# The low part of k as a tile per head with doubled rows, in a two-block transformer of split float32 products

## The chip, the core and the metric

One NeuronCore of one Trainium2 chip runs the whole program in one launch. The metric is device time in microseconds (us), the median of several executions; the kernel before takes 2513.65 us (median of 3, 2512.61 to 2514.68). All inputs and outputs are float32.

## What is computed

512 tokens of 1024 features pass through two blocks. The first has three branches: a forgetting attention of 12 heads of 64 (causal, with a decay taken from gates), a complex diagonal state space model, and attention over 256 memory tokens. The second block is two layers, each with a full attention (8 query heads, 2 key heads of 64), a dilated attention and an MLP of 4096. The change touches the logits of the forgetting and of the dilated attention. Cut to that:

```python
# forgetting attention, per head (12 heads of 64)
s = q @ k.T / 8 + F[:, None] - F[None, :]
s = where(key <= query, s, -1e30)
y = softmax(s) @ v
# dilated attention, per layer: 4 heads of 64 and three groups of (window, dilation)
for (w, d) in ((128, 1), (512, 4), (2048, 16)):
    s = q_g @ k_g.T / 8            # keys at multiples of d within w / 2 of the query
    ...
# the three groups' softmaxes are merged by their log-sum-exp
```

## The kernel before

Every operand of a large product is split into two parts in a rounded float32 format: hi, the rounded value, and lo, the rest. A weight product is three products into one accumulator: hi hi, hi lo, lo hi (`mm3`, L106 to L110; L124 to L126 with tokens as rows). Weights come in pieces of 512 KB: loaded by SP's queue (`fetch`), hi cast by ACT (L88), lo subtracted by DVE or POOL in turn (L90).

A head's logits come twice. The query-major part (`s_item`) makes the row maximum and takes the first product of the pair alone; the key-major part (`t_item`, L365) makes the weights: logits into PSUM (`region_mm`, products at L311), exponential (L379) and cast (L381) on ACT, the low part on DVE (L383), then three products with the values (L400 to L402). In it a head's logits are two products, given by `pairs`:

```python
(qx, own), (kh, kl) = q, k
return [(qx, kh), (qx[own], kl[own])]
```

qx holds hi of q in the head's own 64 rows and lo in the other 64, and kh holds hi of k in both halves, so the first product, with 128 rows, is (q hi + q lo) times k hi. The second is q hi times k lo: 64 rows, 0 to 63 for the first head of a pair and 64 to 127 for the second. `put` (L639) makes these tiles from a finished block of two heads: ACT casts hi (L650), POOL copies it into the other half (L672), DVE subtracts lo (L656). One tile kl serves both heads of a pair, each head in its own rows.

Full attention (`both`) has its own tiles: its second product takes a tile k2, with 128 rows, and is named q,k in the profile. A forgetting unit is two heads with four key blocks each, so 8 products on kl, six units in all. A dilated unit is two heads, each with two tiles of four regions of 128 columns and four tiles of 192 or 256 columns: 24 products on kl; there are two units in each of the two layers. A region in these stretches is the pair, then a bf16 product for the mask (and for the decay, names FM, FF, fk); a key-major tile of the dilated attention begins with a bf16 product for the maximum (L375).

What sets the order: lists of items that `merge` and `mix` deal out among the projections (`layer`: the first dilated unit's key-major items among the branch product `ba`, the second's among the first five gate blocks `gb`), work in the background by `tick`, and behind this a scheduler that reorders the instructions of every engine. Activations live in one ring of 73 tiles of 128x512 (`u`).

Of the kernel before, what the change touches and what calls it, by code (L numbers as in the profile page):

```python
# [10 lines left out]
F32R = mybir.dt.float32r  # L11
# [12 lines left out]
def f32(t):  # L24
    return t.bitcast(F32)


class Core:
# [17 lines left out]
    def u(self, dt=F32, name="u"):  # L46
        """a [128, 512] tile of four-byte words from the common ring."""
        self.n += 1
        return self.ring.tile([128, T], dt, tag="u", name=f"{name}_{self.n}", bufs=self.NU)
# [5 lines left out]
    def psum(self, cfg):  # L55
        """(re)divide the eight PSUM banks"""
        self.psx.close()
        self.PSB = cfg
        self.psx = ExitStack()
        self.n += 1  # L60
        self.ps = self.psx.enter_context(self.tc.tile_pool(name=f"ps{self.n}", bufs=1, space=PSUM))
        self.ctx.push(self.psx)
# [30 lines left out]
    def get(self, name, kb):  # L93
        """the next piece: hi and lo as [128, kb, columns]."""
        i = self.iw
        assert self.strips[i][0] == name, (self.strips[i][0], name)
        for j in range(i, i + self.NW[1]):
            self.split(j)
        for j in range(i + self.NW[1], i + self.NW[1] + self.NW[0]):
            self.fetch(j)  # L100
        self.iw += 1
        n = self.strips[i][1].shape[-1]
        return tuple(t[:, 0:n].rearrange("p (k c) -> p k c", k=kb) for t in self.hl.pop(i))

# [7 lines left out]
    def fm(self, out, w, c0, act, kb):  # L112
        """feature-major block: out[128 features, tokens] from strip columns c0..c0+128."""
# [4 lines left out]
    def tm(self, out, ws, act, tok, cols=slice(0, 256)):  # L118
        """token-major block: out[128 tokens, cols]; ws: pieces that follow one another along k."""
# [34 lines left out]
    @staticmethod  # L154
    def half(t, hf):
        """half of the tokens: of four blocks of 128 in order, two."""
# [3 lines left out]
    def halfp(t, hf):  # L160
        """the first or second half of the tokens, in the order (t mod 4, t div 4)."""
        return t.rearrange("p (r i) -> p r i", r=4)[:, :, 64 * hf:64 * hf + 64]

    def sq_acc(self, xj, j, c=slice(0, T), name="sacc", scale=1.0):
        """sum of squares of the feature blocks, by columns."""
# [11 lines left out]
    def sumcols(self, pq, sacc, cols):  # L177
        """pq[:, i]: sums over features of the tokens of 128-blocks; cols: lists of first columns that add up."""
# [4 lines left out]
    def bcast(self, r):  # L183
        """columns r [128, n] -> [128, n * 128] in PSUM, the same in every row."""
# [7 lines left out]
    def rstd(self, sacc, cols):  # L192
        """broadcast of 1/sqrt(mean + eps), in PSUM."""
# [10 lines left out]
    def hsplit(self, src, bias=None, out=None):  # L204
        """hi, lo of src (+ bias)."""
# [20 lines left out]
class Att(Core):  # L226
    """Softmax attention on split operands. A head's logits come twice: query-major for the row
    maximum, key-major for the weights that multiply V and a block of ones, which sums them."""

    @staticmethod  # L230
    def cut(t, c):
        """columns c of t: a slice, or (i0, i1) for those of the tokens 4 i + r in the order (r, i)."""
# [5 lines left out]
    def byblock(t):  # L238
        """t, tokens 4 i + r in blocks of 128 and within these in the order (r, i), as [p, r, block, i]."""
# [3 lines left out]
    def like(t, c):  # L243
        """t in the shape of the columns c."""
        return t if isinstance(c, slice) else t.rearrange("p (r i) -> p r i", r=4)

    def split3(self, dst, src, nsh):
        """dst[..., i] (bf16, i = 0..2) add up to src (float32)."""
# [15 lines left out]
    def turn(self, mc, psum_tag):  # L264
        """columns [128 tokens, 4, 128] -> rows [128, 512] in PSUM (exact)."""
# [5 lines left out]
    def rows(self, mc, tag, psum_tag, out=None):  # L271
        """the same as bf16 in SBUF; of these the last 32 if out is given."""
# [9 lines left out]
    def unit(self, nh, sregs, tregs, qk, vsl, dst, extra=None, nq=4, hd=64, orow=None, fold=None):  # L282
        """Items of a unit of nh heads (pairs of heads share 128 rows of output).
        sregs(qb): tiles of regions (c0, n, piece, q slice, k slice, mask)
        tregs(): tiles of (regions, [(v piece, kb, columns)])
        fold(j): the tile whose other half takes the rows of -max (else these come by a product of their own)
        qk(j, piece) -> pairs (q, k); vsl(j, piece, kb) -> (hi, lo); dst(j) -> (tile AP rows, row0)"""
# [118 lines left out]
        def vrow(j):  # L406
            """rows of a head's values in its sum; the other half holds the sum of the weights."""
# [41 lines left out]
    def mix(a, b, z=1.0):  # L449
        """a and b as one list, spread evenly, b over the first part z."""  # L450
# [3 lines left out]
    def merge(self, a, b):  # L454
        """run items of a with those of b spread evenly among them."""
# [13 lines left out]
class Blk2(Att):  # L469
    def ada_gen(self, l):  # L470
        """columns [128, 48] of silu(c) @ w_ada[l] + b_ada[l]."""
# [6 lines left out]
        def fin(acc, c):  # L478
            """acc: rows of two parts, c and c + 1"""
# [36 lines left out]
    def load2(self):  # L516
        """constants of the second block"""
# [21 lines left out]
    def norm(self, x, gcols, shcols, h):  # L539
        """by half of the tokens: hi and lo of rms(x) * g + shift. Returns the stages stat, hi, lo."""  # L540
# [24 lines left out]
    def head(self, names, h, posts, norm, view, byw=False):  # L565
        """the first blocks behind a norm, a half of the tokens at a time."""
# [26 lines left out]
    def tail(self, name, act, posts):  # L593
        """the last two blocks before a norm, a half of the tokens at a time."""
# [44 lines left out]
    def put(self, o, isq, dst, scale=None, both=False, byblock=False):  # L639
        """stacks of two heads: q -> [hi;lo]; k -> [hi;hi] and lo in the rows of the head. both: q -> [hi;lo] and hi with  # L640
        the other half left to -max; k -> [hi;hi] and lo with ones for it, for heads of either half."""
# [17 lines left out]
        kl = None  # L659
        for h, (own, oth) in enumerate(((A, B), (B, A))):  # L660
# [23 lines left out]
            if kl is None:  # L684
                kl = self.u(F32R, "kl")
            low(v(kl[own]), o[own], v(f32(hi)[own]))
            dst(h, (hi, kl))
# [7 lines left out]
    def pairs(q, k):  # L695
        """operand pairs whose products make up a head's logits"""
        (qx, own), (kh, kl) = q, k
        return [(qx, kh), (qx[own], kl[own])]
# [12 lines left out]
    def block(self, w, c0, act, kb, post):  # L711
        """one feature-major block; post(psum) may return a generator of later stages."""
# [12 lines left out]
    def strip(self, name, act, kb, posts):  # L725
        """items of feature-major blocks."""
# [12 lines left out]
    def v3(self, nb=4):  # L739
        """hi/lo token-major value tiles [128 keys, nb blocks, 128]."""  # L740
        return tuple(self.u(F32R, "v").rearrange("p (b d) -> p b d", b=nb) for _ in range(2))

    def v_new(self):
        """token-major values of two heads, in two tiles of two key blocks: hi as [v0, 1, 1, v1], lo as [v0, 0, 0, v1]."""
# [8 lines left out]
    def v_put(self, V, src, b0, nb):  # L753
        """src: [128, nb, 128], key blocks from b0."""
# [10 lines left out]
    def tm_items(self, name, act, ncol, evac):  # L765
        """token-major strip: 4 token blocks."""
# [15 lines left out]
    def layer(self, l, norm, view, x, out=None):  # L782
        """norm(h, mod, ada): the stages that fill h; x: the residual tiles (filled by then).
        Returns the new tiles, their squares accumulated, or writes out."""
# [28 lines left out]
        def vpost(key, byblock=False):  # L813
            """values of a feature-major block, transposed"""
# [191 lines left out]
def plan1(out, g, W):  # L1006
    """strips of the first block after u"""
# [45 lines left out]
class Blk1(Blk2):  # L1053
# [21 lines left out]
    def exact_exp(self, out, x):  # L1075
        """exp to float32's accuracy: 2^k * p(x - k ln 2)."""
# [31 lines left out]
    def s5_setup(self):  # L1108
# [21 lines left out]
        # turns, in two parts: uh * t is exact for t < 512  # L1130
# [37 lines left out]
        # powers of a: [., re/im, k, 24]; of its conjugate (k = 0..3) and, for the inputs, k = 4..1  # L1168
# [17 lines left out]
        # four steps at once: phase 4 * (uh + ul), magnitude mag^4  # L1186
# [8 lines left out]
    def s5_mul(self, dst, x, pw, j):  # L1195
        """x * a^k of four pairs, block diagonal: dst[., (pair, k, group, 16)]; rows of a group only in its columns."""
# [15 lines left out]
    def s5_batch(self, j, U, y):  # L1212
        """four pairs of groups, four steps at a time. The state that enters a step is scanned in a frame that
        turns with it; inputs of the same four steps act through a triangular block matrix."""
# [5 lines left out]
        # phases  # L1220
# [13 lines left out]
        # input matrices  # L1234
# [48 lines left out]
        # output matrices  # L1283
# [59 lines left out]
    def forget(self, h, W, bf):  # L1343
# [15 lines left out]
        # ln((1 + a) / 2) = 2 atanh((a - 1) / (a + 3))  # L1359
# [47 lines left out]
    def gate_items(self, name, n, h, G):  # L1407
        """G[j] = z (1 + tanh(z / 2)), twice the gate."""
# [19 lines left out]
    def branch_items(self, br, name, kb, h, y, merged):  # L1428
        """gates run a strip ahead of the projections"""
# [140 lines left out]
    def mem_load(self):  # L1570
        """mem in four tiles of two feature blocks; sums of squares of the even and of the odd blocks."""
# [6 lines left out]
    def mem_prep(self, xm, sacc):  # L1578
        """hi, lo of the normed memory, and the items that fill them."""
# [92 lines left out]
    def s5_out(self, h, ge, ges, merged):  # L1672
# [55 lines left out]
        def norm(h, mod, ada):  # L1728
            """the final norm, and behind it the first one of the next block:
            rms(y) of y = x g r is r sqrt(mean((x g)^2))."""  # L1730
# [45 lines left out]
def cols_of(v):  # L1776
    """[n*128] -> [128, n]"""
# [3 lines left out]
def strips_of(w, kb):  # L1781
    """[kb*128, n*256] -> [n, 128, kb, 256]"""
# [66 lines left out]
def strip_plan(A):  # L1849
    """(name, array, kb) of every weight strip in the order of use; A: the inputs by name, or None for names only."""  # L1850
# [42 lines left out]
def pieces(A):  # L1893
    """(name, array [128, kb * columns] or None, kb, kb * columns) of every piece, in the order of use."""
# [137 lines left out]
```

## Time and profile before

| | |
|---|---|
| median of 3 runs | 2513.65 us (2512.61 to 2514.68) |
| the profiled execution: span, first to last instruction | 2516.8 us (the page gives no other time for it) |
| TensorE products busy | 2388.2 us, 95% of the span, 12162 products |
| TensorE weight loads | 1978.9 us, 79% |
| DVE / ACT / POOL | 61% / 41% / 32% |
| DMA | 265 MB, mean 105 GB/s |
| granted TensorE clock, mean | 0.969 |

How to read it: a product's busy span runs from its start to its modelled end, and the spans of neighbours overlap, so a busy TensorE is not one at its peak; the distance between the starts of products that follow each other tells what one costs. The granted clock is 1.00 at 2.4 GHz and 0.50 at 1.2 GHz. PE is TensorE's products, PEld its weight loads, DVE VectorE, ACT ScalarE, POOL GpSimd, SP the engine that issues the loads.

### The profile page before, as it was taken

How to read it: one execution, taken by the hardware profiler on the slowest of the kernel's cores; microseconds unless marked ns; L12 is line 12 of the kernel's file. 1: busy time of each engine (PE TensorE's matmuls, PEld its weight loads, DVE VectorE, ACT ScalarE, POOL GpSimd, SP SyncE). 2: the span in 40 equal slices, each digit the busy share in tenths (PEclk: the TensorE clock that was granted, in tenths of full speed). 3: DMA queues.
4: the chain of work that ended last, by engine and by line, in shares of the span. 5: the costliest groups of instructions: out<-in, count | busy, mean ns of one | idle time of the engine just before them, and what ended most of it. 6: DMA issues, size and time to landing. Idle time of an engine off the chain costs nothing. (4 is left out here: it accounts for less than half of the span.)

```text
span 2516.8 us, 32068 instructions
## 1 busy us (share of the span) xinstructions
PE 2388.2 (95%) x12162; PEld 1978.9 (79%) x12162; DVE 1533.0 (61%) x2394; ACT 1038.1 (41%) x1639; POOL 812.3 (32%) x601
## 2 busy tenths in 40 slices
PE   7999989989998889999999999998999999999999
PEld 6876778767888777787787888886777777888888
DVE  7667766666998887555459663258864726522222
ACT  4445543452333447533333423433663423423432
POOL 2445354634221552142122121227311612222121
PEclk9999999999998999998899999999999979999999
DMA  5311113213674321121138553233111313222232
GB/s 183 98 47 55 57 61 108 94 59 135 237 264 172 113 76 51 51 85 66 50 102 301 176 209 101 93 114 99 59 51 50 93 34 117 84 94 99 93 101 84
DMA packets 105610, 265.28 MB, mean 105 GB/s; under 512 B 13664, under 2 KB 23408, under 8 KB 105456
## 3 DMA queue, kind: packets, MB, share of 16 engines
q1 hardware_dynamic: 104304, 261.47, 31.2%
q8 instruction: 96, 1.57, 0.3%
q10 hardware_dynamic: 1152, 1.77, 0.2%
q14 instruction: 58, 0.48, 0.1%
HBM read 244.69 MB, written 9.44 MB: 101 GB/s over the span
## 5 line engine op out<-in xcount | busy, mean ns | idle before, releaser
L108 PE MATMUL pmm<-h,wh 128*128 128x512 f32 (+1 forms) x2232 | 855.7, 385 | 14.7 <-ACT h L213 3.9
L110 PE MATMUL pmm<-h,wl 128*128 128x512 f32 (+1 forms) x2232 | 852.9, 382 | 3.7 <-POOL wl L90 2.8
L109 PE MATMUL pmm<-l,wh 128*128 128x512 f32 (+1 forms) x2232 | 853.4, 383 | 0.0
L90 POOL TENSOR_TENSOR wl<-wr,wh 128x1024 fp32r<-128x1024 f32 (+1 forms) x173 | 422.5, 2442 | 1315.4 <-ACT wh L88 1094.4
L88 ACT CAST wh<-wr 128x1024 fp32r<-128x1024 f32 (+1 forms) x346 | 358.2, 1036 | 928.5 <-PE pmm L109 726.4
L108 PEld LDWEIGHTS pmm<-h,wh 128*128 128x128 f32 x2232 | 424.5, 190 | 96.7 <-ACT h L213 4.8
L110 PEld LDWEIGHTS pmm<-h,wl 128*128 128x128 f32 x2232 | 424.5, 190 | 82.5 <-POOL wl L90 3.8
L109 PEld LDWEIGHTS pmm<-l,wh 128*128 128x128 f32 x2232 | 425.2, 191 | 76.5 <-DVE l L221 0.7
L90 DVE TENSOR_TENSOR wl<-wr,wh 128x1024 fp32r<-128x1024 f32 (+1 forms) x173 | 225.1, 1301 | 168.9 <-ACT wh L88 166.5
L383 DVE TENSOR_TENSOR pl<-pe,ph 128x512 fp32r<-128x512 f32 (+4 forms) x168 | 121.7, 733 | 139.7 <-ACT ph L381 138.9
L961 DVE SCALAR_TENSOR_TENSOR x<-pmm,ada,x 128x512 f32<-128x512 f32 (+1 forms) x100 | 64.2, 643 | 213.9 <-PE pmm L110 213.7
L311 PE MATMUL ps<-qk,qk 128*128 128x512 f32 (+4 forms) x416 | 147.9, 386 | 16.1 <-POOL qk L672 9.6
L505 DVE SCALAR_TENSOR_TENSOR adacc<-adw,cact,adacc 128x512 f32<-128x512 f32 x168 | 154.3, 928 | 3.2 <-DMA adw<-in_wada 0.3
L221 DVE TENSOR_TENSOR l<-r,h 128x512 fp32r<-128x512 f32 x64 | 59.3, 928 | 121.6 <-ACT h L213 121.3
L379 ACT ACTIVATE pe<-ps 128x512 f32<-128x512 f32 (+4 forms) x168 | 84.5, 503 | 80.8 <-PE ps L311 72.7
L311 PEld LDWEIGHTS ps<-qk,qk 128*128 128x128 f32 x416 | 83.1, 204 | 37.7 <-POOL qk L672 11.5
L108 PE MATMUL pmm<-yh,wh 128*128 128x512 f32 (+1 forms) x244 | 94.1, 389 | 3.9 <-ACT yh L1403 2.4
L110 PE MATMUL pmm<-yh,wl 128*128 128x512 f32 (+1 forms) x244 | 93.7, 386 | 0.0
L109 PE MATMUL pmm<-yl,wh 128*128 128x512 f32 (+1 forms) x244 | 93.0, 382 | 0.0
L381 ACT CAST ph<-pe 128x512 fp32r<-128x512 f32 (+4 forms) x168 | 88.8, 528 | 9.4 <-DVE pl L383 3.5
L402 PE MATMUL ppv<-pl,v 128*128 128x512 f32 (+2 forms) x216 | 79.0, 366 | 4.1 <-DVE pl L383 4.0
L400 PE MATMUL ppv<-ph,v 128*128 128x512 f32 (+2 forms) x216 | 79.0, 366 | 2.7 <-ACT ph L381 1.6
(365 smaller groups left out, 3863.2 us busy)
## 6 DMA issues: line engine op xcount, KB each, us to landing
wr<-in_w SPq DMA_DIRECT2D x324, 512.0 KB
adw<-in_wada SPq DMA_DIRECT2D x192, 256.0 KB
xs<-xg SPq DMA_DIRECT2D x136, 64.0 KB
wr<-in_w SPq DMA_DIRECT2D x22, 384.0 KB
xd<-x SPq DMA_DIRECT2D x16, 256.0 KB
x<-xd SPq DMA_DIRECT2D x16, 256.0 KB
x<-in_x SPq DMA_DIRECT2D x16, 128.0 KB
x<-in_x SPq DMA_DIRECT2D x8, 256.0 KB
```

Source lines behind the costliest of these rows:

```text
L88: self.nc.scalar.copy(h[:, 0:n], r[:, 0:n])
L90: eng.tensor_tensor(out=l[:, 0:n], in0=r[:, 0:n], in1=f32(h)[:, 0:n], op=ALU.subtract)
L108: mm(out, wh, ah, start=start, stop=False)
L109: mm(out, wh, al, start=False, stop=False)
L110: mm(out, wl, ah, start=False, stop=stop)
L311: mm(outs[i] if len(r.shape) == 2 else outs[i].rearrange("p (r i) -> p r i", r=r.shape[1]), w, r, start=first and i == 0, stop=last and i ...
L379: nc.scalar.activation(out=e[:, w], in_=pt[:, w], func=AF.Exp)
L381: nc.scalar.copy(ph[:, w], e[:, w])
L383: nc.vector.tensor_tensor(out=pl[:, w], in0=e[:, w], in1=f32(ph)[:, w], op=ALU.subtract)
L400: mm(self.cut(pv, c), vh, h, start=f, stop=False)
L402: mm(self.cut(pv, c), vh, lo, start=False, stop=z)
L505: nc.vector.scalar_tensor_tensor(out=acc, in0=w, scalar=cc, in1=acc, op0=ALU.mult, op1=ALU.add)
```

## The change

Every head gets a kl tile of its own. DVE writes its low part into the head's own 64 rows as before, and POOL copies these into the other 64 rows. `pairs` then gives the whole tiles, so the second product has 128 rows: (q hi + q lo) times k lo, which takes in the product of the two low parts as well. Comments and texts that go from the source shift the line numbers behind them by one.

```diff
-        kl = None
         for h, (own, oth) in enumerate(((A, B), (B, A))):
...
-            if kl is None:
-                kl = self.u(F32R, "kl")
+            kl = self.u(F32R, "kl")
             low(v(kl[own]), o[own], v(f32(hi)[own]))
+            nc.gpsimd.tensor_scalar(out=kl[oth], in0=f32(kl)[own], scalar1=1.0, scalar2=0.0, op0=ALU.mult, op1=ALU.add)
             dst(h, (hi, kl))
...
         (qx, own), (kh, kl) = q, k
-        return [(qx, kh), (qx[own], kl[own])]
+        return [(qx, kh), (qx, kl)]
```

TensorE, DVE, ACT and SP have as many instructions as before; POOL has 642 rows in its order instead of 606. The scheduler moves instructions on every engine but SP.

POOL, the first pair of heads of the forgetting attention (qk is the tile of hi, wl the low part of a weight piece, FF and v are filled with constants). Before:

```order
L1383 MEMSET FF 128x1024
L90 TENSOR_TENSOR wl_896<-wr_664,wh_895 128x1024
L672 TENSOR_SCALAR qk_926<-qk_926 64x512
L672 TENSOR_SCALAR qk_931<-qk_931 64x512
L90 TENSOR_TENSOR wl_1164<-wr_833,wh_1163 128x1024
```

With the change:

```order
L1382 MEMSET FF 128x1024
L90 TENSOR_TENSOR wl_896<-wr_664,wh_895 128x1024
L671 TENSOR_SCALAR qk_926<-qk_926 64x512
L685 TENSOR_SCALAR kl_929<-kl_929 64x512
L671 TENSOR_SCALAR qk_932<-qk_932 64x512
L685 TENSOR_SCALAR kl_935<-kl_935 64x512
L90 TENSOR_TENSOR wl_1167<-wr_833,wh_1166 128x1024
```

The copy of the first head's kl stands ahead of the second head's copy of hi, and both copies of kl ahead of the next weight piece.

POOL, the last projections ahead of the second dilated unit of layer 0. Before:

```order
L672 TENSOR_SCALAR qk_10429<-qk_10429 64x512
L672 TENSOR_SCALAR qk_10434<-qk_10434 64x512
L90 TENSOR_TENSOR wl_10588<-wr_10320,wh_10587 128x1024
L672 TENSOR_SCALAR qk_10471<-qk_10471 64x512
L749 MEMSET v_10647 128x2x128
```

With the change:

```order
L671 TENSOR_SCALAR qk_10459<-qk_10459 64x512
L671 TENSOR_SCALAR qk_10465<-qk_10465 64x512
L685 TENSOR_SCALAR kl_10462<-kl_10462 64x512
L685 TENSOR_SCALAR kl_10468<-kl_10468 64x512
L90 TENSOR_TENSOR wl_10624<-wr_10347,wh_10623 128x1024
L671 TENSOR_SCALAR qk_10504<-qk_10504 64x512
L671 TENSOR_SCALAR qk_10510<-qk_10510 64x512
```

Two copies of kl stand ahead of the weight piece and of the last two copies of hi; the last two copies of kl come after the fills that follow.

TensorE, the first key-major tile of the first dilated unit of layer 0 (ppv: products with the values of the full attention; c the constants of the mask). Before:

```order
L311 MATMUL ps_9677<-qk_8636,kl_8783 128x128
L311 MATMUL ps_9677<-qk_8636,qk_8780 128x128
L400 MATMUL ppv_9501<-ph_9536,v_8028 128x512
L401 MATMUL ppv_9501<-ph_9536,v_8032 128x512
L311 MATMUL ps_9677<-qk_8636,kl_8783 128x128
L311 MATMUL ps_9677<-qk_8636,qk_8780 128x128
L402 MATMUL ppv_9501<-pl_9538,v_8028 128x512
L311 MATMUL ps_9677<-qk_8636,kl_8783 128x128
L311 LDWEIGHTS c_3_68
```

With the change:

```order
L311 MATMUL ps_9704<-qk_8657,qk_8801 128x128
L311 MATMUL ps_9704<-qk_8657,kl_8804 128x128
L311 LDWEIGHTS c_3_68
L311 MATMUL ps_9704<-c_3_68 128x512
L400 MATMUL ppv_9528<-ph_9534,v_8046 128x512
L401 MATMUL ppv_9528<-ph_9534,v_8050 128x512
```

The four pairs of the tile now follow one another, and the products with the values come behind the mask. In the second dilated unit of each layer TensorE's order of key-major tiles and products with the values is the same, row for row.

## Rows read from the trace of the kernel before

**Rows 1.** The page, busy time, share of the span and instructions.

```profile
PE 2388.2 (95%) x12162; PEld 1978.9 (79%) x12162; DVE 1533.0 (61%) x2394; ACT 1038.1 (41%) x1639; POOL 812.3 (32%) x601
```

**Rows 2.** Windows: us, busy time per engine, granted clock, DMA share, GB/s.

```profile
116.00:330.00 214.00, 202.77 (x1094) 155.70 (x1094) 159.58 (x251) 110.42 (x200) 99.65 (x103) 0.98 0.17 56
1035.00:1080.00 45.00, 45.00 (x235) 34.57 (x235) 20.37 (x27) 19.33 (x38) 6.03 (x3) 1.00 0.15 48
1180.40:1186.20 5.80, 5.80 (x28) 3.91 (x27) 1.92 (x2) 3.08 (x5) 0.00 (x0) 1.00 0.36 126
1186.20:1210.10 23.90, 23.90 (x83) 18.52 (x83) 4.35 (x9) 9.78 (x24) 0.00 (x0) 0.50 0.00 1
1885.00:1935.00 50.00, 50.00 (x244) 38.22 (x243) 19.59 (x27) 19.87 (x38) 6.27 (x3) 0.93 0.14 48
...
2036.10:2066.80 30.70, 30.70 (x101) 23.27 (x102) 5.47 (x11) 11.46 (x26) 0.00 (x0) 0.50 0.05 16
```

**Rows 3.** Windows of the products on kl alone: busy time, count, granted clock.

```profile
1186.20:1210.10 23.90, 7.04 (x14) 0.50 0.00 1
...
2036.10:2066.80 30.70, 8.92 (x18) 0.50 0.05 16
```

**Rows 4.** Line L311: count, shortest, median and longest ns, first and last start.

```profile
L311 PE MATMUL ps<-qk,kl x144: 322/380/687, 116.1 to 2073.6; 64*128 64x128 f32 x76, 64*128 64x256 f32 x28, 64*128 64x192 f32 x16, 64*128 64x512 f32 x12
```

**Rows 5.** Timeline of TensorE, second dilated unit of layer 0: start, us, form.

```profile
1180.76 0.32 PE L311 MATMUL ps<-qk,kl 64*128 64x128 f32 x1
1181.01 0.33 PE L311 MATMUL ps<-qk,qk 128*128 128x128 f32 x1
1181.27 0.32 PE L311 MATMUL ps<-qk,kl 64*128 64x128 f32 x1
```

**Rows 6.** Timeline of TensorE's weight loads, full attention and second dilated unit.

```profile
946.37 0.19 PEld L311 LDWEIGHTS ps<-q,k 128*128 128x128 f32 x1
...
1181.27 0.18 PEld L311 LDWEIGHTS ps<-qk,kl 64*128 64x128 f32 x1
```

**Rows 7.** Timeline of TensorE, products that all have 128 rows.

```profile
946.36 0.40 PE L311 MATMUL ps<-qk,qk 128*128 128x512 f32 x1
946.60 0.40 PE L311 MATMUL ps<-q,k 128*128 128x512 f32 x1
...
1213.83 0.28 PE L401 MATMUL ppv<-ph,v 128*128 128x128 f32 x1
...
1214.06 0.27 PE L400 MATMUL ppv<-ph,v 128*128 128x128 f32 x1
```

**Rows 8.** Timeline of TensorE in the forgetting attention.

```profile
115.78 0.39 PE L311 MATMUL ps<-qk,qk 128*128 128x512 f32 x1
...
116.53 0.39 PE L311 MATMUL ps<-FM,fk 128*128 128x512 bf16 x1
...
203.50 0.36 PE L311 MATMUL ps<-qk,qk 128*128 128x256 f32 x1
204.10 0.28 PE L311 MATMUL ps<-FM,fk 128*128 128x256 bf16 x1
```

**Rows 9.** Timeline of TensorE at the lower clock, second dilated unit.

```profile
1190.32 0.41 PE L400 MATMUL ppv<-ph,v 128*128 128x128 f32 x1
1190.53 0.41 PE L401 MATMUL ppv<-ph,v 128*128 128x128 f32 x1
...
1192.71 0.47 PE L311 MATMUL ps<-qk,kl 64*128 64x128 f32 x1
...
1193.52 0.47 PE L311 MATMUL ps<-qk,kl 64*128 64x128 f32 x1
```

**Rows 10.** Copies of hi, subtraction of kl (page's groups and line), waits of TensorE.

```profile
L672 POOL TENSOR_SCALAR qk<-qk 64x512 fp32r<-64x512 f32 x40 | 34.9, 873 | 52.1 <-ACT qk L650 35.3 <-PE ps L311 13.3 <-PE pmm L109 0.9
...
L656 DVE TENSOR_TENSOR kl<-xg,qk x24: 672/690/1019, 933.6 to 2003.5; 64x512 fp32r<-64x512 f32 x24
...
PE ps L311 <- POOL qk L672: 9.6, 5, 2.2
```

## The prediction

> **What bounds the kernel now.** I read the page first: TensorE is busy 95% of a span of 2516.8 us [rows 1], so a term counts if it is TensorE's own time, or a wait that TensorE must sit through. Then the busy times by stage, over the five stretches in which the product that is changed occurs [rows 2]. The reader is to see that TensorE is busy for the whole of the stretches of dilated attention (45.00 of 45.00 us, 23.90 of 23.90, 50.00 of 50.00, 30.70 of 30.70), while no engine behind TensorE is busy there for more than 54% of a stretch (ACT, 3.08 of 5.80), and that two of them ran with the granted clock at 0.50, the lower level of 1.2 GHz, although TensorE had been busy without a gap for the 5.80 us before the first fall. The forgetting attention (116 to 330 us) is tighter: TensorE 202.77 of 214, DVE 159.58, POOL 99.65.
>
> Third, the line of the logits' products: 144 products on kl have 64 rows [rows 4], while q,k of full attention, also the second of a pair, has 128 [rows 7]. Of the 144, 48 stand in forgetting attention and 24 in each of the four dilated units. 14 and 18 of them fall into the two stretches at the lower clock [rows 3], 112 elsewhere.
>
> Fourth, the timeline, where starts are to be read, not durations, since busy spans of TensorE overlap. In a dilated unit at 2.4 GHz a pair of 128 columns (qk, then kl) takes from 1180.76 to 1181.27, 0.51 us [rows 5]. Products of the same 128 columns, all with 128 rows, start 0.115 us apart (1213.83 to 1214.06, with one between), and the two of a pair of full attention with 512 columns 0.24 us (946.36, 946.60) [rows 7]. The weight loads say why: the load for q,k starts at 946.37, 0.01 us after the product before it started, so under that product; the load for kl starts at 1181.27, together with its own product and 0.26 us after the product before [rows 5, 6]. A single load is no longer (0.18 against 0.19 us). What costs is that neither it nor the next load gets under a product with another number of rows.
>
> **The sum.** The change gives the 144 products 128 rows; their number, their columns and PSUM use stay.
> (a) At 2.4 GHz. 128 columns: 0.51 - 2 x 0.115 = 0.28 us saved per pair. 512 columns in forgetting attention: qk at 115.78, then kl, the next product at 116.53, so 0.75 for the two [rows 8] against 2 x 0.24 for two of 512 with 128 rows [rows 7]: 0.27. Pairs of 256 columns lie higher: 203.50 to 204.10, 0.60 us [rows 8], where two products of half the columns of the 512 should take 0.24, so 0.36. I take 0.30: 112 x 0.30 = 33.6 us.
> (b) At 1.2 GHz a pair of 128 takes from 1192.71 to 1193.52, 0.81 us [rows 9]. If the clock stays at 2.4 GHz there, it takes 0.23: 32 x 0.58 = 18.6 us.
> (c) The rest of those two stretches is 23.9 + 30.7 - 32 x 0.81 = 28.7 us of other products, which start 0.21 us apart for 128 columns at the lower clock (1190.32, 1190.53) [rows 9], against 0.115: 28.7 x 0.45 = 13 us. The clock fell while TensorE had no idle time but ran pair after pair, and it stayed up in the same kind of unit at 1035 to 1080, where projections lie between the pairs. So I take the pairs for the cause and the clock as returning. The Trainium skill, "TensorE: Matmul & The Clock Gate", section "HAM oscillation — how this bites in real kernels", ties the fall to idle gaps of TensorE; by that rule these gapless stretches would owe it to something else, term (c) would be 0 and (b) smaller, as in the clock's rival. The row of 5.80 busy us in 5.80 does not fit that rule as it stands.
> (a) to (c): 65 us.
> (d) Not all of it is kept in forgetting attention: TensorE already waits 11 us of 214 there and DVE is at 75%, so of its 48 x 0.30 = 14.4 us I keep two thirds: -4.8. In the dilated units nothing else is near full; TensorE is late next itself.
> (e) POOL gets 36 copies of 64x512, the shape and operation of its copies of hi (0.87 us mean, 34.9 us for 40) [rows 10]: 31 us of POOL, which in forgetting attention has 114 us free. Each copy also waits for DVE's subtraction of kl, 0.69 us. Who waits: the key-major products that use kl come after a head's whole query-major part, which uses hi alone, so the copy itself is hidden. What is queued behind it on POOL is not always: in forgetting attention the second head's copy of hi now stands behind the first head's copy of kl; before the second dilated unit two kl copies and a weight split go ahead of the last two copies of hi, as the order shows. TensorE already waited for copies of hi 9.6 us in five waits, the longest 2.2 us [rows 10]. Bounds: 0, if all are covered, and 36 x (0.87 + 0.69) = 56 us if none are. Nearest to the five waits there are, with one copy more each: 5 x 0.87, I take 5 us.
> (f) 18 more tiles are asked of the ring of 73; a wait for a slot would be an ACT or DVE wait, and I price it at 0, with 0 to 11 us (all that TensorE waits in forgetting attention now) as bounds. DVE does the same 36 subtractions as before. The scheduler moves some 850 of 12098 rows on TensorE, mostly projections against attention in forgetting attention and in the first dilated unit; the order of the second dilated unit, where the clock fell, is the same row for row. I give this 0, with 3 us either way.
>
> Sum: 65 - 4.8 - 5 = 55 us. Against the profiled span: 2516.8 - 55 = 2461.8. The page gives no time but the span, which lies 0.13% above the median of 2513.65 of the runs shown; from the median, 2513.65 - 55 = **2459 us**.
>
> **Rivals.** *The clock falls all the same in the two second dilated units.* For it: products of 128 columns with 128 rows are still loads and short products, and after the fall the clock did not come back through runs of such products (rows at 0.21 us). Against: it held through the same runs at 1213 us. Then (c) is 0 and (b) is 32 x (0.81 - 2 x 0.21) = 12.5: 33.6 + 12.5 - 10 = 36 us, 2478.
> *TensorE's gain becomes waits.* With products twice as quick, a unit's exponentials and casts on ACT and subtractions on DVE could be late. Against: ACT is busy 19.33 of 45 and 9.78 of 23.9 us. If half is given back: 28 us, 2486.
> *POOL's queue decides, and the spacing stays.* If the pair is spaced by something else than its rows (by the same accumulator, for instance), or if the products did not in fact take 128 rows, nothing is saved, and the copies on POOL are all that is left: 5 us, 2519, and up to 31 us for 36 exposed copies, 2545, at the places of (e). It decides only then: at 1.56 us per copy with its subtraction, even all 36 exposed come to 56 us, about what the pairs give. Against: full attention's pairs share an accumulator too and start 0.24 us apart. The Trainium skill, "TensorE: Matmul & The Clock Gate", section "LDWEIGHTS (loading the stationary operand)", says that a load's time goes by columns, that of 32 rows being as long as that of 128. The loads of 0.18 and 0.19 us agree; taken as a rule for the whole product it would give this rival, a saving of 0, and the starts 0.51 us per pair against 0.23 speak against taking it so.
> *All is kept:* 65 us and the clock also in 1885 to 1935, where it is 0.93 on the mean: 2445.
>
> **How the numbers follow.** My forecast has 0.66, the clock's rival 0.13, the waits 0.12, all kept 0.03; a tie, where waits and POOL eat nearly everything, 0.03, and POOL's queue 0.03. The range holds the forecast, all that is kept and the clock's rival, and reaches nearly to the waits: 2443 to 2484, which leaves out less than 0.2. Faster by over 0.2% (5 us, about what a measurement of this kernel can tell from no change): 0.94; within: 0.03; slower: 0.03.
>
> **What would show it.** In the changed profile the kl products must have 128 rows, pairs of 128 columns must take about 0.23 us from start to start of the next pair and those of 512 about 0.47, with the kl load under the product before. The granted clock must be 1.00 through both second dilated units, where the work of the 23.9 and 30.7 us then takes about 10 and 13. POOL must show 36 more copies of about 0.87 us, and TensorE's waits for hi at most some 10 us more in all. I am wrong if pairs stay near 0.5 us, if the clock falls to 0.50 there again, or if TensorE's idle time in 116 to 330 us grows by as much as its products shrink.

## The result, and the profile after

The change takes 2488.5 us (2486.96 to 2493.03, 4 runs) where the kernel before took 2513.4 beside it: a ratio of 0.990 (95% interval 0.989 to 0.992), 25 us faster. The forecast was 55 us, with a range that ended at 2484. The profiled execution has a span of 2491.2 us, so 25.6 us less than the 2516.8 of before.

The page, first the busy times, to be read against [rows 1]:

```profile
PE 2343.6 (94%) x12162; PEld 1956.8 (79%) x12162; DVE 1543.0 (62%) x2394; ACT 1036.4 (42%) x1639; POOL 840.3 (34%) x637
```

TensorE's products are 44.6 us shorter, but the span only 25.6: TensorE has more idle time than before. POOL has its 36 further copies in 28.0 us more.

The lines of the products on kl and of the copies (count, shortest, median and longest ns, first and last start), against [rows 4]:

```profile
L311 PE MATMUL ps<-qk,kl x144: 222/276/628, 117.3 to 2050.0; 128*128 128x128 f32 x76, 128*128 128x256 f32 x28, 128*128 128x192 f32 x16, 128*128 128x512 f32 x12
L685 POOL TENSOR_SCALAR kl<-kl x36: 612/630/1476, 89.9 to 2004.6; 64x512 fp32r<-64x512 f32 x36
```

All 144 products have 128 rows, and the median busy span went from 380 to 276 ns. Timeline of TensorE, forgetting attention and second dilated unit of layer 0:

```profile
117.03 0.40 PE L311 MATMUL ps<-qk,qk 128*128 128x512 f32 x1
117.26 0.40 PE L311 MATMUL ps<-qk,kl 128*128 128x512 f32 x1
117.50 0.39 PE L311 MATMUL ps<-FM,fk 128*128 128x512 bf16 x1
...
1198.20 0.28 PE L311 MATMUL ps<-qk,qk 128*128 128x128 f32 x1
1198.32 0.27 PE L311 MATMUL ps<-qk,kl 128*128 128x128 f32 x1
1198.42 0.28 PE L311 MATMUL ps<-qk,qk 128*128 128x128 f32 x1
```

A pair of 128 columns takes 0.22 us (1198.20 to 1198.42; 0.51 in [rows 5]), one of 512 columns 0.47 (117.03 to 117.50; 0.75 in [rows 8]). The weight loads of the same place:

```profile
1198.14 0.19 PEld L311 LDWEIGHTS ps<-qk,qk 128*128 128x128 f32 x1
1198.25 0.19 PEld L311 LDWEIGHTS ps<-qk,kl 128*128 128x128 f32 x1
```

The load for kl starts at 1198.25, under the product that started at 1198.20, where before it started with its own product [rows 6].

Windows over the stretches of [rows 2] (span of the stretch, busy time of TensorE, its loads, DVE, ACT, POOL, granted clock, DMA): forgetting attention, then the four dilated units in order of time.

```profile
116.00:330.00 214.00, 194.53 (x1066) 153.46 (x1065) 150.88 (x237) 107.85 (x195) 100.03 (x107) 0.94 0.16 54
1057.00:1095.00 38.00, 37.37 (x228) 30.57 (x227) 18.83 (x27) 23.54 (x45) 6.30 (x3) 1.00 0.13 42
1196.80:1218.00 21.20, 21.20 (x161) 19.36 (x159) 6.69 (x12) 12.85 (x29) 0.00 (x0) 1.00 0.09 30
1892.00:1927.00 35.00, 35.00 (x221) 29.69 (x221) 17.91 (x24) 18.48 (x37) 6.07 (x3) 1.00 0.14 46
2028.80:2050.00 21.20, 21.20 (x161) 19.36 (x159) 6.69 (x12) 12.85 (x29) 0.00 (x0) 1.00 0.08 29
```

The dilated units behave as forecast, the clock at 1.00 in both second units. The forgetting attention doesn't: TensorE is idle 19.5 of 214 us (before 11.2), and its clock is 0.94, not 0.98.

Where the time went is read best from a mark that both kernels pass in the same order. ACT casts 346 weight pieces; the starts of the 49th (behind the forgetting attention), the 129th and the 137th (around the end of the first layer's full attention), the 161st (behind the second dilated unit) and the 345th. Before:

```profile
423.64 1.05 ACT L88 CAST wh<-wr 128x1024 fp32r<-128x1024 f32 x1 [11.19 <-PE pmm L109]
...
959.48 1.04 ACT L88 CAST wh<-wr 128x1024 fp32r<-128x1024 f32 x1
...
1052.01 1.05 ACT L88 CAST wh<-wr 128x1024 fp32r<-128x1024 f32 x1 [0.63 <-PE pmm L109]
...
1266.30 1.04 ACT L88 CAST wh<-wr 128x1024 fp32r<-128x1024 f32 x1
...
2491.00 1.05 ACT L88 CAST wh<-wr 128x1024 fp32r<-128x1024 f32 x1 [4.43 <-PE pmm L109]
```

With the change:

```profile
433.96 1.05 ACT L88 CAST wh<-wr 128x1024 fp32r<-128x1024 f32 x1 [9.65 <-PE pmm L109]
...
969.27 1.05 ACT L88 CAST wh<-wr 128x1024 fp32r<-128x1024 f32 x1 [0.42 <-PE pmm L109]
...
1073.59 1.04 ACT L88 CAST wh<-wr 128x1024 fp32r<-128x1024 f32 x1
...
1265.68 1.04 ACT L88 CAST wh<-wr 128x1024 fp32r<-128x1024 f32 x1
...
2465.52 1.05 ACT L88 CAST wh<-wr 128x1024 fp32r<-128x1024 f32 x1 [4.43 <-PE pmm L109]
```

So the change is 10.3 us late behind the forgetting attention, where some 10 us were to be gained; it stays so up to the 129th cast (9.8); it loses 11.8 more by the 137th (21.6 late), a stretch that is mostly full attention; then it gains 22.2 by the 161st, and 24.9 after that. Two losses of about 10 to 12 us, neither of them in the forecast, face gains close to those forecast.

**The first loss.** Waits of TensorE, 116 to 330 us (line waited for: us in total, times, longest), with the change; pl is the low part of the attention's weights, which DVE makes:

```profile
PE ppv L402 <- DVE pl L383: 7.4, 4, 3.0
PE ppv L400 <- ACT ph L381: 2.7, 4, 0.9
PE ps L311 <- DVE unm L336: 2.2, 3, 1.1
PE ps L311 <- POOL qk L671: 1.5, 1, 1.5
```

Before, there is no wait for pl in this stretch. Around the longest the clock falls as well, as the windows show:

```profile
160.00:165.00 5.00, 4.93 (x37) 4.20 (x35) 4.97 (x7) 1.30 (x3) 3.88 (x6) 1.00 0.23 90
165.90:168.90 3.00, 0.00 (x0) 0.00 (x0) 2.91 (x6) 0.86 (x3) 1.90 (x3) 0.74 0.00 0
167.40:168.90 1.50, 0.00 (x0) 0.00 (x0) 1.44 (x4) 0.00 (x0) 0.40 (x1) 0.50 0.00 0
169.00:175.60 6.60, 6.29 (x29) 4.42 (x29) 3.87 (x10) 2.75 (x5) 0.00 (x0) 0.61 0.00 0
```

TensorE stands for 3.00 us, DVE being at other work (2.91 us busy) before it gets to pl; within that gap the clock falls to 0.50, and most of the 6.6 us behind it run at the lower level. Here the rule of the Trainium skill, "TensorE: Matmul & The Clock Gate", section "HAM oscillation — how this bites in real kernels", that idle gaps of TensorE bring the clock down, fits the row in kind: a gap, and the clock down within it. How long a gap has to be, no run here shows.

**The second loss.** Windows, before, of the stretch between two projections at the end of layer 0's full attention: all instructions, then those on pmm, the projections' tile, alone.

```profile
978.20:989.30 11.10, 9.12 (x40) 5.55 (x39) 9.41 (x13) 10.81 (x20) 1.65 (x2) 1.00 0.15 47
978.20:989.30 11.10, 0.00 (x0) 0.00 (x0) 0.00 (x0) 0.53 (x1) 1.00 0.15 47
```

The same with the change:

```profile
984.70:1009.20 24.50, 17.88 (x64) 10.50 (x62) 17.97 (x25) 19.44 (x34) 4.32 (x5) 0.89 0.06 21
984.70:1009.20 24.50, 0.01 (x1) 0.31 (x1) 0.00 (x0) 0.60 (x1) 0.89 0.06 21
```

With the change TensorE goes 24.5 us without a projection to fill the attention's gaps, instead of 11.1, is idle 6.6 us of it and has a clock of 0.89. No product on kl lies there. Beside the order, two of the copies are new there:

```profile
1001.46 1.63 POOL L685 TENSOR_SCALAR kl<-kl 64x512 fp32r<-64x512 f32 x2
```

The runs below show the same stretch without any copy.

### The profile page after: what moved, and what is told of

Same layout as the page of the kernel before. It is cut to its first block, busy times and chain, and to the rows that moved or that the text cites. A ratio compares the mean times of both kernels' runs of the same rounds, so it can differ in the third digit from the quotient of the medians.

```text
span 2491.2 us, 32131 instructions
## 1 busy us (share of the span) xinstructions
PE 2343.6 (94%) x12162; PEld 1956.8 (79%) x12162; DVE 1543.0 (62%) x2394; ACT 1036.4 (42%) x1639; POOL 840.3 (34%) x637
## 4 chain that ended last, share of the span: by engine, by line
PE 47%; DVE 7%; issue 3%; ACT 2%; DMA 2%; POOL 2%; SPq 1%; DVEq 0%; POOLq 0%; ACTq 0%
PE pmm L108 13%; PE pmm L109 13%; PE pmm L110 13%; PE ps L311 3%; DMA adw<-in_wada 1%; PE ppv L400 1%; PE ppv L402 1%; PE ppv L401 1%; POOL wl L90 1%; DMA xs<-xg 1%; DVE unm L336 1%; DVE xs L624 0%; ACT qk L650 0%; DVE adacc L505 0%; DVE rs L430 0%
## 5 line engine op out<-in xcount | busy, mean ns | idle before, releaser
L311 PE MATMUL ps<-qk,qk 128*128 128x512 f32 (+4 forms) x416 | 143.9, 380 | 21.8 <-POOL qk L671 9.1
L311 PEld LDWEIGHTS ps<-qk,qk 128*128 128x128 f32 x416 | 81.2, 200 | 43.9 <-POOL qk L671 11.3
L336 DVE TENSOR_REDUCE unm<-ps 128x1 f32<-128x512 f32 (+2 forms) x112 | 64.7, 596 | 31.3 <-PE ps L311 30.8
```

Source lines behind the costliest of these rows:

```text
L311: mm(outs[i] if len(r.shape) == 2 else outs[i].rearrange("p (r i) -> p r i", r=r.shape[1]), w, r, start=first and i == 0, stop=last and i ...
L336: nc.vector.tensor_reduce(out=nm, in_=pts[0], axis=AX.X, op=ALU.max, negate=True)
```

## The experiments

The theory at the start: the 128 rows are worth what was forecast, and something that comes with the copies (their time on POOL, the 18 further tiles, or the new order of the instructions) costs 25 to 30 us. The rival: TensorE's gain itself turns into waits for DVE and falls of the clock. All runs were timed in five rounds beside the kernel before; ratios are to that.

**The rows without the copies (e4_shared_tile).**

```diff
-            kl = self.u(F32R, "kl")
+            if kl is None:
+                kl = self.u(F32R, "kl")
             low(v(kl[own]), o[own], v(f32(hi)[own]))
-            nc.gpsimd.tensor_scalar(out=kl[oth], in0=f32(kl)[own], scalar1=1.0, scalar2=0.0, op0=ALU.mult, op1=ALU.add)
...
         return [(qx, kh), (qx, kl)]
```

> The kernel of before with one edit: pairs gives the whole tiles, and kl stays one tile for both heads of a pair, with no copies and no further tiles. The second product then has 128 rows, its own head's 64 as before and the low part of q times the low part of the other head's k, a term of the size of the roundings that are left out. Every engine has the instructions of before in the order of before. Theory A (the rows are worth what was forecast, about 55 to 65 us; the loss of some 25 to 30 us comes with the copies on POOL, the further tiles and the new order of the instructions): 2450 to 2465 us, no new waits for pl in the forgetting attention. Theory B (the rows are TensorE's gain, but it turns into waits for DVE and falls of the clock whatever the order is): within 6 us of the change, 2483 to 2495 us.

Measured: 2458.6 us, ratio 0.978 (0.975 to 0.981), 55 us faster than before and about 30 faster than the change. This is the best version of the study, and the one to keep.

**The copies without the rows (e3_copies_alone).**

```diff
-        return [(qx, kh), (qx, kl)]
+        return [(qx, kh), (qx[own], kl[own])]
```

> The change with pairs as before: a kl tile per head and the 36 copies on POOL stay, but the second product has 64 rows and nobody reads the copies. All engines have the instructions of the change in the order of the change. Theory A (copies and order cost 25 to 30 us by themselves): 2535 to 2545 us. Theory B (the loss is TensorE's gain turned into waits): within 6 us of before, 2508 to 2520 us.

Measured: 2537.7 us, ratio 1.009 (1.006 to 1.012), 23 us slower. The two runs make a square with before and the change. The rows give 55 us in the order of before, and 1.009 - 0.990 = 0.019 or 47 us in the order of the change; all that comes with the copies costs 23 us with 64 rows and about 31 (0.990 - 0.978) with 128. The loss is there without any gain of TensorE, and in the run of the rows alone the gain is there without the loss, so the rival is out as the main cause. Whether the rows are worth less in the order of the change (47 against 55 us) lies within the intervals.

**By place (e1_dilated_only, e2_forgetting_only).** The change in the dilated units alone, and in the forgetting attention alone: `put` and `pairs` take a flag.

```diff
+            if dbl:
+                kl = self.u(F32R, "kl")
...
+        if not dbl:
+            return [(qx, kh), (qx[own], kl[own])]
         return [(qx, kh), (qx, kl)]
```

> The change in the dilated units alone (24 copies, 96 products of 128 rows); the forgetting attention as before, in the order of before up to the first layer. Theory A: the 11 us that the change lost in the forgetting attention are gone, the 12 us lost in the first layer's full attention, whose order still moves, may stay: 2472 to 2482 us. Theory B: the same for the forgetting attention, and the loss in the first layer stays for certain: 2475 to 2480 us. The run tells mainly whether the two losses are independent of each other; if the first layer's loss is gone too, it came from the forgetting attention: 2462 to 2468 us.

Measured: 2482.1 us, ratio 0.987 (0.985 to 0.990).

> The change in the forgetting attention alone (12 copies, 48 products of 128 rows); the dilated units as before. Either theory: slower than before by the 11 us seen at the end of the forgetting attention, 2520 to 2530 us, with the TensorE waits for pl of 7 us or more at 116 to 330 us. If it comes out at 2508 to 2516 us, the loss seen there is made good later, and the loss in the first layer is independent of it.

Measured: 2525.5 us, ratio 1.004 (1.002 to 1.007). In the first of them the 129th cast is 0.6 us ahead of before and the 137th 9.8 late; in the second the 49th cast is 9.1 late, and from there nothing more is lost. The two losses are independent, each with the tiles and copies of its own place.

**Tiles or copies (e5_tiles_alone, e6_copies_to_scratch).** First a tile per head, with 64 rows and no copies:

```diff
-            nc.gpsimd.tensor_scalar(out=kl[oth], in0=f32(kl)[own], scalar1=1.0, scalar2=0.0, op0=ALU.mult, op1=ALU.add)
...
-        return [(qx, kh), (qx, kl)]
+        return [(qx, kh), (qx[own], kl[own])]
```

> Before with a kl tile for each head (18 more tiles asked of the ring) and nothing else: products of 64 rows, no copies on POOL. The instructions' order comes out near that of the change (199 of 12097 TensorE rows differ from it, 1649 from before). Theory C (the copies on POOL are what costs 23 us): 2510 to 2520 us. Theory R (the further tiles in the ring, and the order that follows from them, are what costs): 2530 to 2542 us, with the loss at the end of the forgetting attention and at the end of the first layer's full attention, as in the run of the copies alone.

Measured: 2532.8 us, ratio 1.007 (1.004 to 1.011).

Then, from the kernel with the shared tile, copies to a place outside the ring:

```diff
+            if h == 0:
+                sc = self.t(self.base, [128, T], BF16, "kc", 1)
+            nc.gpsimd.tensor_scalar(out=sc[oth], in0=f32(kl)[own], scalar1=1.0, scalar2=0.0, op0=ALU.mult, op1=ALU.add)
```

> The shared tile with products of 128 rows, and the 36 copies on POOL put back, but into one scratch tile (bf16) outside the ring that nobody reads: POOL has the work of the change, the ring has the tiles of before. 598 TensorE rows move against before. Theory C: 2478 to 2486 us. Theory R: 2455 to 2466 us.

Measured: 2465.0 us, ratio 0.981 (0.977 to 0.985). So tiles without copies lose 18 of the 23 us that tiles and copies lose with 64 rows, and copies without tiles little (0.981 against 0.978, intervals that overlap). In the run with tiles alone the second loss stands as in the change, while the 49th cast is on time (0.1 us late). The same stretch between two projections, tiles alone:

```profile
974.80:999.40 24.60, 18.00 (x62) 10.50 (x61) 17.92 (x25) 19.43 (x34) 2.79 (x3) 0.89 0.07 21
974.80:999.40 24.60, 0.00 (x0) 0.33 (x1) 0.00 (x0) 0.60 (x1) 0.89 0.07 21
```

**The ring (e7_ring_70, e11_ring_74).** The kernel with the shared tile and another ring; for 74, `s5t` has 10 buffers instead of 12.

```diff
-    NU = 73
+    NU = 70
```

> The shared tile with products of 128 rows, no copies, and a ring of 70 tiles instead of 73: about as many fewer as the doubled tiles of one set of dilated projections take. The order is that of before up to TensorE row 2101, behind the forgetting attention, and in the layers it comes nearer to that of the change. Theory R: the gain in the forgetting attention stays, the 12 us at the end of the first layer's full attention are lost: 2467 to 2478 us. Theory C, in which neither ring nor order matters: 2455 to 2463 us.

Measured: 2468.9 us, ratio 0.983 (0.980 to 0.987).

> The shared tile with products of 128 rows, no copies, and a ring of 74 tiles instead of 73 (two of the twelve small buffers of 128x24 of the state space model's setup are given up for the space). The order in the forgetting attention is that of before, in the layers 580 TensorE rows move. If the ring is what is short in the first layer's full attention, one more tile gains there or does no harm: ratio to before 0.974 to 0.979, 2450 to 2461 us. If it is the given order that happens to be good, and any other is worse: 0.980 to 0.987, 2464 to 2480 us.

Measured: 2466.2 us, ratio 0.979 (0.977 to 0.981): neither better nor worse than with 73 (the ratio lies in the first range expected, the time in the second). With 70 the stretch without a projection is back:

```profile
963.20:988.60 25.40, 18.64 (x68) 10.81 (x69) 17.92 (x27) 21.06 (x36) 3.20 (x3) 0.96 0.06 21
```

With 74 it isn't:

```profile
977.90:989.20 11.30, 9.15 (x41) 5.64 (x39) 9.40 (x13) 11.00 (x20) 1.64 (x2) 1.00 0.14 46
```

So the length of that stretch goes with the number of free tiles: some 11 us with 73 or 74 and the shared tile (11.10 in the run of the rows alone too), some 25 with 70, or with 73 and a tile per head. From the 129th to the 137th cast the kernel takes 101.3 us with 70 and 89.4 with 74. In the forgetting attention the order of TensorE, DVE and ACT didn't move with 70.

**Order alone (e8_order_of_change).** The shared tile again, no copies; after the kernel is written down, every instruction of TensorE, DVE and ACT gets an order-only edge to the one ahead of it in the order that the change has:

```diff
         mixer_kernel(tc, out, **args)
+        pin(nc, tc)
...
+        for x, y in zip(o, o[1:]):
+            tc.add_manual_dep(by[e][y], by[e][x].name, info, reason="pin")
```

> The shared tile with products of 128 rows, no copies, no further tiles, a ring of 73: the kernel that took 2458.6 us, but TensorE, DVE and ACT are held, instruction by instruction, in the order that the scheduler gave the change (a table of numbers with order-only edges). Theory O (the order alone costs the 25 to 30 us; that a ring slot is waited for or POOL copies on the chip costs nothing): 2482 to 2492 us, with the loss at the end of the forgetting attention and of the first layer's full attention. Theory S (the order is harmless; slots that come free late and copies that come late on the chip cost): 2455 to 2466 us. Between: 2466 to 2482, each has its part.

Measured: 2482.4 us, ratio 0.986 (0.984 to 0.987; the kernel before took 2520.5 beside it), so 19 us of the 31 are the order by itself, with some 8 us either way (an estimate from the two intervals). The second loss is there in full: from the 129th to the 137th cast this kernel takes 102.6 us, the change 104.3, the shared tile in its own order 89.4, so 13 of the 19 us lie there. The 49th, 129th and 137th cast in the order of the change:

```profile
427.93 1.05 ACT L88 CAST wh<-wr 128x1024 fp32r<-128x1024 f32 x1 [9.60 <-PE pmm L109]
...
963.32 1.05 ACT L88 CAST wh<-wr 128x1024 fp32r<-128x1024 f32 x1 [0.40 <-POOL qk L672]
...
1065.88 1.05 ACT L88 CAST wh<-wr 128x1024 fp32r<-128x1024 f32 x1
```

The same casts with the shared tile in its own order (e4_shared_tile):

```profile
416.58 1.05 ACT L88 CAST wh<-wr 128x1024 fp32r<-128x1024 f32 x1 [9.61 <-PE pmm L109]
...
951.04 1.04 ACT L88 CAST wh<-wr 128x1024 fp32r<-128x1024 f32 x1
...
1040.41 1.05 ACT L88 CAST wh<-wr 128x1024 fp32r<-128x1024 f32 x1
```

The edges cost nothing there by themselves: held by the same edges in the order of before (e10_scratch_held, below), the kernel takes 89.3 us from the 129th to the 137th cast.

The waits for pl are there too, 90 to 430 us:

```profile
PE ppv L402 <- DVE pl L383: 7.6, 6, 2.7
```

In the kernel with the shared tile in the order of before the same line is:

```profile
PE ppv L402 <- DVE pl L383: 0.2, 1, 0.2
```

**The forgetting attention in its old order (e9_forgetting_order).** The change, held in the same way in the order of before for that stage alone; the table `ORDER`, from which the edges are made, is cut to it.

```diff
         mixer_kernel(tc, out, **args)
+        pin(nc, tc)
```

> The change as it is, with its tiles and copies, but in the forgetting attention TensorE, DVE and ACT are held in the order of before (TensorE's first 1780 products, DVE's first 360 and ACT's first 300 instructions; from there the scheduler is free, and the layers get the order of the run with the change in the dilated units alone). Theory O: the 10 us lost and the 7 us not gained in the forgetting attention come back, the first layer's loss stays: 2468 to 2476 us. Theory S: 2484 to 2492 us, the forgetting attention still ends some 10 us later than before.

Measured: 2489.3 us, ratio 0.988 (0.987 to 0.990). This missed theory O and lies in the range of theory S: 5 us better than the change at most, and not surely so. The 49th cast is 5.1 us late instead of 10.3, but 12.2 behind the kernel with the shared tile. The old order alone didn't bring the forgetting attention back while the tiles and copies are there.

**Copies alone, order held (e10_scratch_held).** The copies to scratch, with TensorE, DVE and ACT held in the order of before by the same call and its own table.

```diff
         mixer_kernel(tc, out, **args)
+        pin(nc, tc)
```

> The kernel of the copies to scratch (shared tile, products of 128 rows, 36 copies on POOL that nobody reads), with TensorE, DVE and ACT held in the order of before by a table. What is left against the kernel of 2458.6 us is the copies alone: 36 x 0.8 us of POOL and what stands behind them there. Theory O (POOL's copies are covered): ratio to before 0.976 to 0.980, about 2456 to 2463 us. Theory C' (the copies cost the 5 us of the prediction's step e, without any new order): 0.980 to 0.983, 2463 to 2472 us, with the difference in the forgetting attention.

Measured: 2470.0 us, ratio 0.981 (0.978 to 0.983), about 7 us more than without copies; the intervals overlap, so a cost of the copies alone is not shown clear of the noise. Its windows, 90 to 430 us:

```profile
90.00:430.00 340.00, 304.46 (x1654) 248.63 (x1663) 241.89 (x374) 157.03 (x270) 174.19 (x176) 0.95 0.20 63
```

Against the shared tile without copies:

```profile
90.00:430.00 340.00, 308.96 (x1759) 255.34 (x1758) 244.23 (x381) 161.45 (x276) 169.69 (x166) 0.97 0.21 68
```

About a hundred products fewer are done in the same time, at a lower clock. In this execution the 49th cast is 11.6 us later than with the shared tile alone, from the 49th to the 137th another 1.0. In the run of the order alone it is 11.3 us later, in the change 17.4.

These three sizes are soft, for they are single executions and that of the shared tile was the fastest of its six. The run with a ring of 74 has the shared tile, no copies and, up to 408 us, the order of before; its 49th cast and its window are:

```profile
423.98 1.05 ACT L88 CAST wh<-wr 128x1024 fp32r<-128x1024 f32 x1 [9.65 <-PE pmm L109]
90.00:430.00 340.00, 308.99 (x1698) 253.54 (x1698) 240.50 (x377) 159.45 (x273) 167.24 (x165) 0.94 0.20 63
```

That is 7.4 us later than with 73, with the same 31.0 us of idle time on TensorE and a clock of 0.94 instead of 0.97; with a ring of 70 the cast starts at 412.35. So among three executions with no copies and, in this stage, the same order of TensorE, DVE and ACT the mark moves by some 12 us. Against the latest of the three, the order alone and the copies alone are each about 4 us late and the change 10: that both together lose time here is borne out, how much each loses is not.

## Why the prediction was wrong

**Step (a), the price of the rows: right.** Pairs take 0.22 us where 0.23 was forecast, those of 512 columns 0.47 where 0.48 (2 x 0.24). The run of the rows alone gave 55 us in its median and 64 in its profiled execution; (a) to (c) made 65.

**Steps (b) and (c), the clock in the second dilated units: right.** The clock is 1.00 in both. From the first to the last product on kl they took 37.6 and 40.5 us before (1180.8 to 1218.4, 2033.1 to 2073.6), and 21.2 and 21.2 now: 35.7 us gained. The steps gave 18.6 + 13 + 16 x 0.30 for the pairs outside the slow stretches = 36.4. So the pairs of 64 rows were the cause of the fall there: with the copies alone, which differ from the change in these rows only and have its order, the clock fell again in both units:

```profile
1203.20:1236.50 33.30, 33.30 (x160) 25.96 (x159) 6.70 (x12) 12.91 (x29) 0.00 (x0) 0.80 0.05 17
2052.30:2090.00 37.70, 37.70 (x161) 29.52 (x159) 6.70 (x12) 13.05 (x29) 0.00 (x0) 0.68 0.05 16
```

The rule of the Trainium skill on idle gaps, as the prediction weighed it, would have made (c) 0; the runs decide against that for these stretches. The Trainium skill, "TensorE: Matmul & The Clock Gate", section "A second HAM failure mode: psum-queue depth-cycling", also tells of short idle times between groups of products that make the clock swing; the starts 0.26 us apart where 0.115 is enough might hide such times, since ends of products are modelled, but no run here shows them.

**Step (d), two thirds kept in the forgetting attention: wrong in sign, for another reason.** With the rows alone it gained 7.1 us (forecast 9.6, less the share of (e)); the two other executions without copies in this order, with rings of 70 and 74, give a gain of 11.3 and a loss of 0.3. With the change it lost 10.3. Waits for DVE, which the step had in mind, came, but not from a quicker TensorE alone: in 116 to 330 us those for pl are 0.2 us with the rows alone, 4.3 in the order of the change with 64 rows (copies alone), and 7.6 in that order with 128 rows (order alone).

**Step (e), POOL's queue: size open, wrong in mechanism.** It priced 5 us; the copies alone show about 7, not clear of the noise. But the waits for hi that were to grow are 9.1 us in five with the change, 9.6 in five before [rows 10]. A copy itself was 0.78 us in the mean (28.0 / 36), not 0.87.

**Step (f), the failed step: "a wait for a slot ... I price it at 0" and, of the scheduler's moves, "I give this 0, with 3 us either way".** These two zeros were one thing. Eighteen more tiles in a ring without room made the scheduler write another order, and that order by itself costs 19 us. The step looked for the price of a full ring as waits of ACT or DVE in the trace; it is paid for the most part in the order, and lies in part where the change has no product (the full attention of layer 0; two of its copies stand there, but the loss is the same without any). The prediction counted some 850 moved rows on TensorE. That the second dilated unit was unmoved was read as good news for (c), rightly, but nothing was asked of the places that did move: whether projections still lie between attention products there.

**The rivals.** The clock's rival is out. "TensorE's gain becomes waits" came near in time (2486), by luck: the loss and waits for pl come with 64 rows too, and with the rows alone the gain is kept. One sign of being wrong that the prediction named couldn't fail to come: in a window of fixed length (116 to 330 us) idle time grows by exactly what busy time shrinks, here 8.2 us. "POOL's queue decides, and the spacing stays" is out.

The account, in ratios to before: rows -0.022; order +0.0075 (0.9855 - 0.978); copies +0.003, within the noise; the change as a whole -0.010. Of the 31 us between the change and the shared tile 19 are shown as order. The intervals of the order alone (0.984 to 0.987) and of the change (0.989 to 0.992) don't overlap, so the tiles and copies cost something beyond the order, some 12 us; how much of it is the copies (the 7 us above) and how much slots that come free late stays open. Why the scheduler holds the projections back when tiles are short, which allocation it waits for, was not traced. Whether the change could run in the order of before through the whole program was not tried.

## What to carry to other kernels

Equal row counts in neighbouring products are worth 0.28 to 0.29 us a pair here, and more where uneven pairs bring the clock down; look first for a form that fills the rows with what is there already (here the other head's low part, whose product with the low part of q is of the size of the roundings left out), not with a copy. A buffer more from a pool that has no room is not free because nobody waits for it: compare the order of instructions, and count how long TensorE goes without filler work in each moved stretch. To split a change into its work and its reordering, hold the order of one version with order-only edges and run the other.

## What was not expected of the hardware

A gap of 3.00 us was followed by a further loss: within it the clock fell to 0.50, and the 6.6 us behind it ran at a mean of 0.61. That the gap brought the fall is read from this order in time and was not tested by itself. Over 90 to 430 us the mean clock is 0.97 with the shared tile and 0.93 with the change:

```profile
90.00:430.00 340.00, 305.34 (x1632) 246.96 (x1630) 240.73 (x370) 155.93 (x269) 173.85 (x176) 0.93 0.19 62
```

As an estimate from these rounded means, 340 x 2 x 0.03 = 20 us against 340 x 2 x 0.07 = 48 us lie at the level of 0.50: 28 us more at half the pace, which costs some 14 us at most. So falls of the clock can carry most of the 17.4 us by which the two differ behind the forgetting attention. Part of that can be the execution and not the change: with the shared tile and a ring of 74, the same order gave 0.94 and a mark 7.4 us later, at equal idle time.
